# Hybrid DiT forward on one core: dead tiles as load buffers of the expert weights, row transposes one product later, routing in pieces

## The chip, the cores and the metric
One core of a Trainium2 chip runs the whole program. Its engines are PE (matrix products), ACT, DVE, POOL (element by element work, and POOL's indirect transfers) and SP, which issues the weight loads; 16 DMA engines move the data. The metric is the device time of one execution in microseconds (us); lower is better.

## The reference
Two transformer layers on 512 latent tokens of width 1024 and 256 context tokens, all in float32. Layer 0 mixes by a convolution and neighbourhood attention and has a dense feed-forward. Layer 1 mixes by windowed and differential attention, and its feed-forward is a mixture of eight experts, of which each token takes two. The change touches the second half of layer 1:

```python
def swiglu(x, w1, w3, w2):
    return (jax.nn.silu(x @ w1) * (x @ w3)) @ w2
...
    logits = (xt @ router).astype(jnp.float32)
    top_v, top_i = lax.top_k(logits, TOP_K)
    top_w = jax.nn.softmax(top_v, axis=-1)
    gates = jnp.sum(jax.nn.one_hot(top_i, N_EXPERTS, dtype=jnp.float32) * top_w[..., None], axis=1)
...
    for e in range(1, N_EXPERTS):
        out = out + gates[:, e:e + 1] * swiglu(xt, w1[e], w3[e], w2[e])
...
        h = h + g1 * y
        h = h + g2 * ffn(rms_norm(h, norm2_g[l]) * (1 + sc2) + sh2)
```
An expert has w1 and w3 of 1024 x 1408 and w2 of 1408 x 1024.

## The kernel before
**Numbers in halves.** Each float32 weight block is split into two float16 halves, `whi` on ACT (line 269) and the rest `wlo` on DVE (line 274); PE forms three float16 products for each block of 128 rows (`mm1`, line 342).

**The weight stream.** `Stream` walks a list of blocks in the order in which PE wants them. An expert has 11 blocks `m13` (128 x 2048, 1 MB, two tiles of w1 and w3) and 8 blocks `m2` (128 x 1408, 704 KB). `load_to` issues loads on SP (line 246) into buffers of the kind 'st'; `split_to` makes the halves in buffers of the kind 'hl', and each split issues the load that may use the place; `get` splits up to `ls` blocks ahead of PE (5 among the experts). The buffer of block i follows from i modulo their number. Among the experts there are five 'st' (two of the pool, `wst`, two of a further pool, `wstx`, and a third of the dead normed-activation tile `aT3`) and eight 'hl' (four, two `whix`/`wlox`, and two thirds of `aT3`). A buffer's name in a row is that of the pool or tile that it lies in, so a row `aT<-wst` is a split too. Blocks in the set `fine` are split in four pieces of 512 columns.

**The norm and the routing.** Behind the attention's output product the residual `h` is complete; the sum of its squares (ACT, line 453) goes through a small chain for the root on DVE (lines 321 to 333), then `n` is formed on DVE and ACT (lines 421, 419), and PE transposes it (`nps`, line 431) and computes the router's logits. `route` then ranks the tokens on DVE: eight fixed places ("slots") with capacities 176, 192, 96, 176, 112, 152, 136 and 128 take the eight experts. For each slot one-hot rows `ohs` (line 1684) and small PE products (`idxps`) give the token of each place; `idx`, the target row `sidx` and the weight `ws` follow by small DVE operations for each slot and half, and `cmax` (line 1790) says whether any expert has more tokens than places. SP reads `cmax` in its queue (line 1904) to decide on an overflow loop, which doesn't run on these inputs.

**An expert.** Its rows come from memory by indirect transfers on POOL (`gather`, line 1796; `xg`), are transposed by PE (`xtp`, line 1821), scaled (`xaf`, line 1825) and split into `xT`; this `prep` for expert e+1 is issued after block j = 6 of expert e. For expert 0, PE makes `xT` by products with one-hot rows instead (line 1817). Then eleven blocks j: 48 products each into a PSUM tile `mps` (three buffers), emptied one block later by `evac`: ACT's silu `ms` (line 1847), DVE's `mgf` (line 1848), and for j = 3, 7, 10 the halves `mgT` (lines 1853, 1854). Then eight blocks d of w2: 33 products each, and `evac2`: ACT's `my` (line 1876), PE's transposes `ytp` (line 1880), DVE's weighting into `yr` (line 1884). After d = 7, in the last expert after d = 4 and d = 7, POOL adds the rows to the result in memory (line 2019). A capacity over 128 needs two row halves: 128 and the rest.

**What sets the order.** The program order is that of the code, rearranged by a scheduler that fills each engine's instruction list; each engine then runs its list in order, and waits where an operand isn't there.

## Time and profile before
| | us |
|---|---|
| three runs, median (lowest to highest) | 1785.67 (1781.9 to 1789.2) |
| the profiled execution | 1788.69 |
| its span, first to last instruction | 1786.8 |
| PE busy in the span | 1668.7 |
| DVE busy in the span | 1251.0 |
| ACT busy in the span | 883.1 |

The mean granted TensorE clock of the profiled execution is 0.977. The span is what the rows below are counted in; what lies around it is 1.9 us. Busy time of an engine is a sum over stages with different limits, so it is read stage by stage.

### The profile page before, as it was taken

The numbers are of one execution on the slowest core, as the hardware profiler recorded it, in microseconds if no ns is written. First come the engines' busy times: TensorE is split into PE (matmuls) and PEld (weight loads), VectorE is DVE, ScalarE is ACT, GpSimd is POOL, SyncE is SP. The second block draws the span as 40 slices with busy tenths as digits, with TensorE's granted clock in tenths as the row PEclk, the third lists the DMA queues.
The fourth block names the chain that finished last, engine by engine and source line by source line (L and its number), as shares of the span: only waits on it lengthen the run. The fifth ranks groups of instructions, "written<-read, shape, count | busy, mean of one in ns | idle before, by whom it ended". The sixth has DMA issues, their size and how long they took to land. (4 is left out here: it accounts for less than half of the span.)

```text
span 1786.8 us, 36195 instructions
## 1 busy us (share of the span) xinstructions
PE 1668.7 (93%) x15124; PEld 1170.3 (65%) x15124; DVE 1251.0 (70%) x2463; ACT 883.1 (49%) x1420; POOL 156.1 (9%) x102
## 2 busy tenths in 40 slices
PE   3999999999999999999999999989789999999997
PEld 1444666555566665555555466447579988989997
DVE  6784899877665444333147999696898588788884
ACT  6564555262222222111254667564666577677773
POOL 1100000000000000000000000451210113101201
PEclk9999999999999999999999999999799999999999
DMA  8413342534333442233312201101569788899893
GB/s 322 160 51 100 104 166 95 212 117 143 142 129 131 142 142 96 73 112 112 115 61 79 95 1 48 70 3 54 189 204 337 240 312 334 303 330 336 313 337 109
DMA packets 51801, 286.82 MB, mean 161 GB/s; under 512 B 5824, under 2 KB 10944, under 8 KB 27568
## 3 DMA queue, kind: packets, MB, share of 16 engines
q1 hardware_dynamic: 47328, 271.74, 41.8%
q0 software_dynamic: 3296, 10.95, 2.7%
q8 instruction: 120, 1.97, 0.4%
q10 hardware_dynamic: 1008, 1.77, 0.3%
q14 instruction: 49, 0.40, 0.1%
HBM read 272.57 MB, written 11.08 MB: 159 GB/s over the span
## 5 line engine op out<-in xcount | busy, mean ns | idle before, releaser
L342 PEld LDWEIGHTS <-whi 128*128 128x128 f16 x5184 | 469.7, 99 | 185.3 <-issue 10.8
L342 PE MATMUL f<-yT,whi 128*128 128x512 f16 (+1 forms) x1408 | 325.5, 326 | 1.5 <-ACT af L438 1.5
L342 PEld LDWEIGHTS <-wlo 128*128 128x128 f16 x2592 | 255.6, 99 | 90.4 <-issue 2.2
L274 DVE SCALAR_TENSOR_TENSOR wlo<-wst,whi 128x512 f16<-128x512 f32 (+2 forms) x154 | 236.8, 1549 | 68.1 <-ACT whi L269 67.6
L269 ACT ACTIVATE whi<-wst 128x2048 f16<-128x2048 f32 (+2 forms) x152 | 199.4, 1331 | 111.1 <-PE f L342 72.8
L342 PE MATMUL f<-yT,wlo 128*128 128x512 f16 (+1 forms) x704 | 229.1, 326 | 0.0
L375 DVE SCALAR_TENSOR_TENSOR adjk<-wst,srow 128x1024 bf16<-128x1024 f32 x96 | 117.3, 1221 | 98.4 <-DMA wst<-in_w_adr_dram 97.2
L342 PE MATMUL f<-gT,whi 128*128 128x512 f16 (+1 forms) x704 | 164.4, 326 | 0.0
L342 PE MATMUL mps<-xT,whi 128*128 128x176 f16 (+6 forms) x1472 | 149.0, 229 | 3.8 <-DVE mgf L1848 3.7
L342 PE MATMUL mps<-xT,wlo 128*128 128x176 f16 (+6 forms) x736 | 143.0, 229 | 0.0
L342 PE MATMUL f<-gT,wlo 128*128 128x512 f16 (+1 forms) x352 | 114.7, 326 | 0.0
L342 PEld LDWEIGHTS <-aT 128*128 128x128 f16 x1584 | 106.8, 99 | 5.3 <-issue 4.5
L467 DVE TENSOR_TENSOR h<-h,ytp 128x256 f32<-128x256 f32 (+1 forms) x48 | 24.3, 507 | 109.2 <-PE ytp L465 108.9
L2019 POOL DMA_INDIRECT out_dram<-yr,sidx x14 | 54.4, 3885 | 358.3 <-DVE yr L1884 215.3
L342 PE MATMUL cvps<-aT,whi 128*128 128x512 f16 (+1 forms) x384 | 82.6, 328 | 2.8 <-ACT Kl L632 2.3
L342 PEld LDWEIGHTS <-whix 128*128 128x128 f16 x992 | 81.4, 98 | 2.9 <-issue 2.5
L1082 ACT CAST gT<-g 128x512 f16<-128x512 f32 (+1 forms) x23 | 14.0, 608 | 131.0 <-DVE g L1079 131.0
L274 DVE SCALAR_TENSOR_TENSOR wlo<-wstx,whi 128x2048 f16<-128x2048 f32 (+2 forms) x42 | 68.7, 1651 | 14.0 <-ACT whi L269 11.4
L342 PE MATMUL mps<-xT,aT 128*128 128x176 f16 (+6 forms) x1056 | 74.4, 231 | 2.3 <-DVE mgf L1848 2.3
L342 PE MATMUL mps<-mgT,whi 128*128 128x176 f16 (+6 forms) x704 | 73.0, 227 | 0.9 <-ACT mgT L1853 0.9
L342 PE MATMUL mps<-mgT,wlo 128*128 128x176 f16 (+6 forms) x352 | 68.1, 227 | 0.0
L269 ACT ACTIVATE whi<-wstx 128x2048 f16<-128x2048 f32 (+2 forms) x42 | 57.7, 1401 | 17.6 <-PE mps L342 16.3
(398 smaller groups left out, 3490.1 us busy)
## 6 DMA issues: line engine op xcount, KB each, us to landing
wst<-in_w_m_dram SPq DMA_DIRECT2D x38, 1024.0 KB, 6.2
wstx<-in_w_m_dram SPq DMA_DIRECT2D x33, 1024.0 KB, 6.2
wst<-in_w_adr_dram SPq DMA_DIRECT2D x32, 1024.0 KB, 4.9
wst<-in_w_f_dram SPq DMA_DIRECT2D x22, 1024.0 KB, 4.8
wst<-in_w_m_dram SPq DMA_DIRECT2D x27, 704.0 KB, 6.0
wstx<-in_w_m_dram SPq DMA_DIRECT2D x25, 704.0 KB, 6.1
aT<-in_w_m_dram SPq DMA_DIRECT2D x17, 1024.0 KB, 6.2
wst<-in_w_ada_dram SPq DMA_DIRECT2D x12, 1024.0 KB, 4.9
```

Of the source, the lines that this page charges most:

```text
L269: nc.scalar.activation(h, x, AF.Copy, scale=self.scale)
L274: nc.vector.scalar_tensor_tensor(out=l, in0=x, scalar=SW, in1=h, op0=OP.mult, op1=OP.subtract)
L342: mm(ps[:, s0:s0 + sn], w[:, k, :], a[:, kk, s0:s0 + sn], start=first and p == 0, stop=last and p == 2)
L375: nc.vector.scalar_tensor_tensor(out=jk, in0=st[:, j * D:(j + 1) * D], scalar=1.0, in1=self.srow[:, t, :], op0=OP.mult, op1=OP.mult, accum ...
L467: nc.vector.tensor_tensor(out=hs, in0=hs, in1=tp[:, 0:w].rearrange("p (t c) -> p t c", t=nt), op=OP.add)
L1082: nc.any.tensor_copy(gh, g[:, 0:sn])
L2019: self.nc.gpsimd.indirect_dma_start(out=to, out_offset=bass.IndirectOffsetOnAxis(ap=self.sidx[0:sn, e, s:s + 1], axis=0), in_=yr[0:sn, s, ...
```

## The change
Five things are edited.

1. **Load buffers.** The tiles of the queries `Qc` and of the keys `Kd`, dead after the attention, are kept and serve as three 'st' buffers as soon as the differential attention is done; behind the routing the dead residual tile `h` gives three more. All three parts of `aT3` become 'hl' buffers, the further pool gives one 'hl' alone. That makes eight of each kind (2 + 3 + 3, and 4 + 1 + 3). A block takes the buffer that was used longest ago.
2. **Even halves.** A capacity over 128 is cut in two equal halves (88 + 88, 96 + 96, 76 + 76, 68 + 68), each with a `yr` tile of its own.
3. **Rows later.** `evac2` only makes `my`; the transposes and `yr` (now `rows`) come one block d later.
4. **Split start of w2.** Products of d = 0 and d = 1 run over k = 0 to 7 first, then over k = 8 to 10.
5. **Routing in pieces.** Only slots 0 and 1 are done ahead of expert 0. The one-hot rows of the others, the targets and weights of all slots in one go, and `cmax` (`excess`) are called from expert 0's loop over j (`beside`).

```diff
     def slot(self, i, kind, cols):
-        n = self.ns if kind == 'st' else self.nb
-        more = self.more.get(kind, []) if i < self.more_end else []
-        r = i % (n + len(more)) - n
-        if r >= 0 and more[r] is not None:
-            return [z[:, 0:cols] for z in more[r]]
-        pool, n, x = (self.pool, n, '') if r < 0 else (self.more_pool, more.count(None), 'x')
+
+        e = min((z for z in self.slots[kind] if z[0] == 'base' or i < self.more_end), key=lambda z: z[2])
+        where, pool, last = e
+        e[2] = i
+        if where not in ('base', 'pool'):
+            assert last < (self.nsplit if kind == 'st' else self.pos), (kind, i, last)
+            return [z[:, 0:cols] for z in pool]
+        x = '' if where == 'base' else 'x'
+        n = sum(z[0] == where for z in self.slots[kind])
...
-            T['cq'] = lp.tile([128, 8, NL], F16, name="Qc")
+            T['cq'] = self.kp.tile([128, 8, NL], F16, name="Qc")
             T['ck'] = lp.tile([128, 3, NT], F16, name="Kc")
-            T['dk'] = lp.tile([128, 12, NT], F16, name="Kd")
+            T['dk'] = self.kp.tile([128, 12, NT], F16, name="Kd")
...
+                qk = [T['cq'].rearrange("p a t -> p (a t)")]
+                kd = T['dk'].rearrange("p a t -> p (a t)")
+                qk += [kd[:, 4 * D * z:4 * D * z + 4 * D] for z in range(2)]
+                self.wfix = [fixed_slot('st', f"qk{i}", z) for i, z in enumerate(qk)]
+                self.S.extend(fixed=self.wfix)
+                self.S.load_to(self.S.nsplit + self.S.depth())
...
-        for s in range(1, NE):
-            tokens(s, slots(s, lambda t: ps_[:, s - 1, t:t + 1]))
-            if s == 1:
-                self.gather(1)
...
+        tokens(1, slots(1, lambda t: ps_[:, 0, t:t + 1]))
+        for i, (s0, sn) in enumerate(self.slots[1]):
+            V.tensor_copy(self.idx[0:sn, 1, i:i + 1], ip[0:sn, 1, i, 0:1])
+        self.gather(1)
+
+        def rest(j):
+
+            if j == 0:
+                tokens(0, first)
+            elif 2 <= j + 1 < NE:
+                s = j + 1
+                tokens(s, slots(s, lambda t: ps_[:, s - 1, t:t + 1]))
+                if s == 2:
+                    for i, (s0, sn) in enumerate(self.slots[s]):
+                        V.tensor_copy(self.idx[0:sn, s, i:i + 1], ip[0:sn, s, i, 0:1])
+            elif j + 1 == NE:
+
+                to = rp.tile([128, 8, 2], F32, name="to")
+                V.tensor_copy(self.idx[:, 3:NE, :], ip[:, 3:NE, :, 0])
+                V.tensor_scalar(to, ip[:, :, :, 1], -1.0, 1.0, op0=OP.mult, op1=OP.add)
+                V.tensor_tensor(out=to, in0=to, in1=own.unsqueeze(2).broadcast_to([128, 8, 2]), op=OP.mult)
+                V.tensor_tensor(out=to, in0=to, in1=ip[:, :, :, 0], op=OP.add)
+                V.tensor_scalar(to[:, NE - 1, :], to[:, NE - 1, :], 8.0, None, op0=OP.mult)
+                V.tensor_copy(self.sidx, to)
+                V.tensor_reduce(out=self.ws, in_=ip[:, :, :, 2:4], axis=AX.X, op=OP.add)
+            elif j == NE:
+                excess()
...
+            if beside is not None:
+                beside(j)
...
-        yr = mp.tile([128, max(2, len(slots)), D], F32, name="yr", tag="yr", bufs=1)
+        yr = [mp.tile([128, D], F32, name="yr", tag=f"yr{s}", bufs=1) for s in range(len(slots))]
         py = []
 
         def evac2():
             d, ps = py.pop(0)
-            y = mp.tile([128, cm], F32, name="my", tag="my", bufs=2)[:, 0:C]
+            y = mp.tile([128, cm], F32, name="my", tag="my", bufs=nb)[:, 0:C]
             nc.scalar.activation(y, ps[:, 0, 0:C], AF.Copy, scale=gate[:, d, 0:1])
+            ys.append((d, y))
+
+        def rows():
+            d, y = ys.pop(0)
             tp = pp.tile([128, max(2, len(slots)), 128], F32, name="ytp", tag="t", bufs=2)
             dd = slice(d * 128, (d + 1) * 128)
             for s, (s0, sn) in enumerate(slots):
                 nc.tensor.transpose(tp[0:sn, s, :], y[:, s0:s0 + sn], self.ident)
                 if wt is None:
-                    nc.vector.tensor_copy(yr[0:sn, s, dd], tp[0:sn, s, :])
+                    nc.vector.tensor_copy(yr[s][0:sn, dd], tp[0:sn, s, :])
                 else:
-                    nc.vector.tensor_scalar(yr[0:sn, s, dd], tp[0:sn, s, :], wt[0:sn, s:s + 1], None, op0=OP.mult)
+                    nc.vector.tensor_scalar(yr[s][0:sn, dd], tp[0:sn, s, :], wt[0:sn, s:s + 1], None, op0=OP.mult)
             done(d, yr)
 
+        def part(w, ps, ks):
+            for k in ks:
+                self.mm1(ps[:, 0], *w, k, gT[:, 0], gT[:, 1], seg, k == 0, k == 10)
+
+        ys = []
+        w0 = []
         for d in range(8):
-            wh, wl = (z.rearrange("p (k c) -> p k c", k=11) for z in w2(d))
+            if d > 1 and len(ys) > nb - 1:
+                rows()
+            w = [z.rearrange("p (k c) -> p k c", k=11) for z in w2(d)]
             ps = pp.tile([128, 2, CB], F32, name="mps2", tag="m", bufs=3)
-            for k in range(11):
-                self.mm1(ps[:, 0], wh, wl, k, gT[:, 0], gT[:, 1], seg, k == 0, k == 10)
+            if d < 2 and nb > 1:
+
+                part(w, ps, range(8))
+                w0.append((w, ps))
+                if d == 0:
+                    continue
+                for i in range(2):
+                    part(*w0[i], range(8, 11))
+                    py.append((i, w0[i][1]))
+                evac2()
+                continue
+            part(w, ps, range(11))
             if py:
                 evac2()
             py.append((d, ps))
         evac2()
+        while ys:
+            rows()
...
-        self.slots = [[(0, min(C, 128))] + ([(128, C - 128)] if C > 128 else []) for C in CAPS]
+
+        self.slots = [[(0, C // 2), (C // 2, C // 2)] if C > 128 else [(0, C)] for C in CAPS]
         self.eid = {}
...
-            self.S.extend(wx, 2, 2)
+            self.S.extend(wx, 0, 1, fixed=self.wfix)
...
-                self.S.extend(wx, 2, 2, fixed=[fixed_slot(k, z) for k, z in zip(BUSE, B)])
+                H = [self.ht[:, 2 * D * z:2 * D * z + 2 * D].bitcast(F16) for z in range(3)]
+                self.S.extend(wx, 0, 1, fixed=self.wfix + [fixed_slot('hl', f"a{i}", z) for i, z in enumerate(B)]
+                              + [fixed_slot('st', f"h{i}", z) for i, z in enumerate(H)])
```

`excess` holds the removed lines from `cb` to `cmax`, unchanged. Line numbers in the rows of the changed order are those of the changed file, 14 to 63 higher.

What moves is seen at three places of the engines' lists. First DVE at the norm ahead of the routing; `sst` is the sum of squares, `rs_v`, `rs_r` and `rs_t` the chain of the root, `n_3` the normed rows. Before:

```order
L324 TENSOR_SCALAR rs_v<-rs_v 128x2 [waits DVE_49]
L329 SCALAR_TENSOR_TENSOR rs_t<-rs_r,rs_v 128x1 [waits DVE_49]
L329 SCALAR_TENSOR_TENSOR rs_t<-rs_r,rs_v 128x1
L333 SCALAR_TENSOR_TENSOR rs_r<-rs_t,rs_r 128x2 [waits DVE_49]
L329 SCALAR_TENSOR_TENSOR rs_t<-rs_r,rs_v 128x1 [waits DVE_49]
L329 SCALAR_TENSOR_TENSOR rs_t<-rs_r,rs_v 128x1
L333 SCALAR_TENSOR_TENSOR rs_r<-rs_t,rs_r 128x2 [waits DVE_49]
L329 SCALAR_TENSOR_TENSOR rs_t<-rs_r,rs_v 128x1 [waits DVE_49]
L329 SCALAR_TENSOR_TENSOR rs_t<-rs_r,rs_v 128x1
L333 SCALAR_TENSOR_TENSOR rs_r<-rs_t,rs_r 128x2 [waits DVE_49]
L421 TENSOR_SCALAR n_3_13519<-h_11895,rs_r 128x512 [waits DMAHW1_49,DMAHW2_49,DVE_49,Pool_49]
```

And of the change, from the same instruction on:

```order
L338 TENSOR_SCALAR rs_v<-rs_v 128x2 [waits DVE_49]
L288 SCALAR_TENSOR_TENSOR wlo_14097<-Qc,whi_14096 128x512 [waits DMAHW1_49,Activation_49]
L343 SCALAR_TENSOR_TENSOR rs_t<-rs_r,rs_v 128x1 [waits DVE_49]
L343 SCALAR_TENSOR_TENSOR rs_t<-rs_r,rs_v 128x1
L288 SCALAR_TENSOR_TENSOR wlo_14097<-Qc,whi_14096 128x512 [waits Activation_49]
L347 SCALAR_TENSOR_TENSOR rs_r<-rs_t,rs_r 128x2 [waits DVE_49]
L288 SCALAR_TENSOR_TENSOR wlo_14097<-Qc,whi_14096 128x512 [waits Activation_49]
L343 SCALAR_TENSOR_TENSOR rs_t<-rs_r,rs_v 128x1 [waits DVE_49]
L343 SCALAR_TENSOR_TENSOR rs_t<-rs_r,rs_v 128x1
L288 SCALAR_TENSOR_TENSOR wlo_14097<-Qc,whi_14096 128x512 [waits Activation_49]
L347 SCALAR_TENSOR_TENSOR rs_r<-rs_t,rs_r 128x2 [waits DVE_49]
```

Four pieces of a split of a weight block (in `Qc`; block 7 of expert 0) now stand inside the chain; three instructions of the root and `n_3` follow. ACT's list at the same place, of the change:

```order
L467 ACTIVATE sqj,ssq_11906<-h_11901 128x128 [waits DVE_49,Activation_49]
L467 ACTIVATE sqj,ssq_11906<-h_11901 128x128 [waits Activation_49]
L283 ACTIVATE whi_14096<-Qc 128x512 [waits DMAHW1_49]
L283 ACTIVATE whi_14096<-Qc 128x512 x3
L433 ACTIVATE n_3_13527<-h_11901,rs_r 128x512 [waits DMAHW4_49,DMAHW5_49,DVE_49,Pool_49]
L433 ACTIVATE n_3_13527<-h_11901,rs_r 128x512
```

The first two rows are the last sums of squares, and `n_3` is ACT's part of the normed rows; before, nothing stood between them. The four pieces of `whi` moved in, the first with a wait for a transfer.

Second, PE in expert 0. Of the change:

```order
L356 MATMUL mps<-xT,whi_13259 128x176
L356 LDWEIGHTS whi_13351
L356 MATMUL mps<-xT,whi_13351 128x176
L1858 MATMUL xtp<-ident,xg_13924 128x96 [waits DMASW4_49]
L1858 MATMUL xtp<-ident,xg_13924 128x96
L356 LDWEIGHTS whi_13171
L356 MATMUL mps<-xT,whi_13171 128x176 [waits DVE_49]
L356 LDWEIGHTS wlo_13172
L356 MATMUL mps<-xT,wlo_13172 128x176
```

`xg` are the gathered rows of expert 1, `xtp` their transposes. These two stand behind the first 39 products of expert 0 (`mps<-xT`), with a wait for the gather. Before, all sixteen stood behind block j = 2:

```order
L342 MATMUL mps<-xT,whi_13342 128x176
L342 LDWEIGHTS wlo_13343
L342 MATMUL mps<-xT,wlo_13343 128x176
L1821 MATMUL xtp<-ident,xg_13918 128x128 [waits DMASW4_49,Activation_49]
L1821 MATMUL xtp<-ident,xg_13918 128x64 [waits DMASW5_49]
L1821 MATMUL xtp<-ident,xg_13918 128x128
L1821 MATMUL xtp<-ident,xg_13918 128x64
L1821 MATMUL xtp<-ident,xg_13918 128x128 [waits Activation_49]
```

Fourteen of the sixteen moved back, behind block j = 6, and two moved forward.

Third, ACT behind the routing, of the change (`sw` is the scale of a split, `xaf` and `xT` the operand of expert 0):

```order
L283 ACTIVATE whix_13930<-Kd,sw 128x512 x2
L1862 ACTIVATE xaf<-xtp,nB_106,nA_102 128x176 [waits PE_49]
L283 ACTIVATE whix_13930<-Kd,sw 128x512
L1865 CAST xT<-xaf 128x704 [waits DVE_49,Activation_49]
L1862 ACTIVATE xaf<-xtp,nB_106,nA_102 128x176 [waits PE_49]
L283 ACTIVATE aT_13066<-Kd,sw 128x512 x2
L1862 ACTIVATE xaf<-xtp,nB_106,nA_102 128x176 [waits PE_49]
L283 ACTIVATE aT_13066<-Kd,sw 128x512 x2
L283 ACTIVATE aT_13066<-wst_13181,sw 128x512 x4
L1865 CAST xT<-xaf 128x704 [waits DVE_49,Activation_49]
```

The second CAST of `xT`, which was on DVE before, stands here behind the pieces of splits of blocks 4 and 5.

## Rows read from the trace of the kernel before
**Rows 1.** The page, parts 1 and 2: busy time of each engine, and the bytes moved in 40 equal slices of 44.7 us each. The expert part is slices 29 to 40.
```profile
PE 1668.7 (93%) x15124; PEld 1170.3 (65%) x15124; DVE 1251.0 (70%) x2463; ACT 883.1 (49%) x1420; POOL 156.1 (9%) x102
GB/s 322 160 51 100 104 166 95 212 117 143 142 129 131 142 142 96 73 112 112 115 61 79 95 1 48 70 3 54 189 204 337 240 312 334 303 330 336 313 337 109
```

**Rows 2.** Stretches of 50 us of the expert part, all engines. Columns: stretch, length, then busy us (and number of instructions) of PE, PEld, DVE, ACT, POOL, the granted TensorE clock, the DMA share, GB/s.
```profile
1300.00:1350.00 50.00, 43.66 (x507) 41.02 (x506) 45.66 (x152) 30.97 (x44) 6.13 (x5) 0.90 0.73 245
...
1450.00:1500.00 50.00, 45.01 (x823) 41.09 (x822) 38.80 (x44) 37.23 (x49) 8.49 (x4) 0.90 0.89 310
...
1700.00:1750.00 50.00, 48.57 (x802) 46.79 (x800) 44.82 (x50) 37.02 (x42) 4.41 (x2) 1.00 0.94 337
```

**Rows 3.** Waits of PE between 1255 and 1787 us: who waited <- for whom: us in total, times, longest us.
```profile
PE mps L342 <- DVE mgf L1848: 8.7, 8, 3.7
PE ytp L1880 <- ACT my L1876: 5.4, 12, 1.1
...
PE mps L342 <- ACT mgT L1853: 1.9, 5, 0.5
PE ytp L1880 <- DVE yr L1884: 1.9, 8, 0.4
```

**Rows 4.** PE's timeline, places in expert 0 and the begin of its second product (`mgT`). Columns: start us, us, engine, line, operation, out<-in, count, and in brackets the idle time before and what ended it.
```profile
1313.00 3.35 PE L1821 MATMUL xtp<-ident,xg 128*128 128x128 f32 x12 [0.19 <-ACT xaf L1825]
1318.47 3.82 PE L342 MATMUL mps<-xT,aT 128*128 128x176 f16 x25 [2.12 <-DVE mgf L1848]
...
1339.04 0.31 PE L342 MATMUL mps<-xT,whi 128*128 128x176 f16 x2 [3.75 <-DVE mgf L1848]
...
1355.24 1.98 PE L342 MATMUL mps<-mgT,aT 128*128 128x176 f16 x24
```

**Rows 5.** Stretches of 5 us, columns as in rows 2.
```profile
1310.00:1315.00 5.00, 4.67 (x39) 3.44 (x37) 5.00 (x52) 2.19 (x5) 0.00 (x0) 1.00 0.01 3
...
1335.00:1340.00 5.00, 1.25 (x17) 1.11 (x15) 5.00 (x5) 4.12 (x7) 0.00 (x0) 0.99 0.77 246
1340.00:1345.00 5.00, 5.00 (x47) 5.00 (x45) 5.00 (x6) 2.97 (x3) 0.00 (x0) 0.67 0.92 297
1345.00:1350.00 5.00, 5.00 (x69) 5.00 (x67) 3.80 (x5) 3.40 (x5) 0.00 (x0) 1.00 0.94 330
...
1475.00:1480.00 5.00, 5.00 (x64) 4.91 (x65) 3.06 (x4) 3.10 (x6) 2.49 (x2) 0.51 0.72 254
1480.00:1485.00 5.00, 5.00 (x121) 5.00 (x118) 3.42 (x4) 3.94 (x5) 0.00 (x0) 1.00 0.70 224
```

**Rows 6.** Groups of instructions between 1240 and 1360 us. Columns: line, engine, operation, out<-in, out<-in shapes, count, then busy us, mean ns of one, idle before.
```profile
L274 DVE SCALAR_TENSOR_TENSOR aT<-wst,aT 128x512 f16<-128x512 f32 x8 | 5.2, 676 | 0.0
...
L1848 DVE SCALAR_TENSOR_TENSOR mgf<-mps,ms 128x176 f32<-128x176 f32 x11 | 3.6, 335 | 1.7 <-ACT ms L1847 1.7
...
L274 DVE SCALAR_TENSOR_TENSOR wlo<-wstx,whi 128x2048 f16<-128x2048 f32 x1 | 2.3, 2285 | 0.0
...
L1684 DVE TENSOR_SCALAR ohs<-cstm,pms 128x128 f16<-128x128 f32 x4 | 0.9, 273 | 0.0
...
L269 ACT ACTIVATE whi<-wst 128x512 f16<-128x512 f32 x16 | 9.1, 624 | 3.6 <-DMA wst<-in_w_m_dram 2.4 <-PE odps L342 1.2
```

**Rows 7.** Timelines of DVE and PE at the norm ahead of the routing, columns as in rows 4.
```profile
1273.22 0.16 DVE L476 TENSOR_REDUCE sst<-ssq 128x2 f32<-128x6 f32 x1 [0.30 <-ACT sqj L453]
...
1275.57 0.16 DVE L333 SCALAR_TENSOR_TENSOR rs_r<-rs_t,rs_r 128x2 f32<-128x2 f32 x1
1275.82 0.88 DVE L421 TENSOR_SCALAR n<-h,rs_r 128x512 f32<-128x512 f32 x2
...
1276.45 1.09 PE L431 MATMUL nps<-ident,n 128*128 128x128 f32 x4 [3.22 <-DVE n L421]
```

**Rows 8.** SP's timeline and its wait, which hold the load queue (SPq); the first rows as in rows 4, the last as in rows 3.
```profile
1267.91 0.33 SPq L246 DMA_DIRECT2D wst<-in_w_m_dram  x1
...
1299.23 0.33 SPq L246 DMA_DIRECT2D aT<-in_w_m_dram  x1
1315.45 3.07 SPq L246 DMA_DIRECT2D wst<-in_w_m_dram  x2
...
SPq L1904 <- DVE cmax L1790: 13.8, 1, 13.8
```

**Rows 9.** PE's and ACT's timelines where expert 2 (96 places) runs, columns as in rows 4.
```profile
1467.73 1.38 ACT L269 ACTIVATE aT<-wstx 128x1408 f16<-128x1408 f32 x1 [1.83 <-DMA wstx<-in_w_m_dram]
1469.55 0.71 PE L1821 MATMUL xtp<-ident,xg 128*128 128x128 f32 x2 [1.42 <-ACT xaf L1825]
```

**Rows 10.** POOL's timeline at the first gather, columns as in rows 4, and from the view of the tile `xg` the time from issue to landing of all 11 gathers (1300 to 1591 us).
```profile
1300.22 1.24 POOL L1796 DMA_INDIRECT xg<-n_d,idx  x1 [12.62 <-DVE ohs L1684]
...
DMA to landing us min/median/max: 4.6/5.8/8.4
```

**Rows 11.** Timelines of DVE and POOL at the end of the last expert, columns as in rows 4.
```profile
1769.29 0.35 DVE L1884 TENSOR_SCALAR yr<-ytp,ws 128x128 f32<-128x128 f32 x1 [1.61 <-PE ytp L1880]
1771.24 0.35 DVE L1884 TENSOR_SCALAR yr<-ytp,ws 128x128 f32<-128x128 f32 x1 [1.60 <-PE ytp L1880]
...
1771.88 1.59 POOL L2019 DMA_INDIRECT out_dram<-yr,sidx  x1 [27.11 <-DVE yr L1884]
1778.05 1.56 POOL L2019 DMA_INDIRECT out_dram<-yr,sidx  x1 [4.58 <-DMA out_dram<-yr,sidx]
```

106 lines of the change are left out of this document (55 added, 51 removed).

## The prediction
> **What bounds the kernel now.** I began with the busy times. PE works 93% of the span, DVE 70%, ACT 49% [rows 1], so PE is the bound wherever it doesn't stop, and a change that leaves its matmuls alone can only give back PE's stops and the time it spends at a low clock. The edit leaves everything up to about 1250 us in its order, so the question is the expert part alone, 1297 to 1776 us. Read in stretches of 50 us [rows 2], a good one has 48.57 us of PE; only two fall short: 1300 to 1350 (43.66, granted clock 0.90) and 1450 to 1500 (45.01, clock 0.90). DMA is close behind PE in the good ones (337 GB/s, share 0.94), so in this part the weight stream is the second bound.
>
> Then the waits of PE by name [rows 3]: `mgf` 8.7 us in 8 stops, of which two in expert 0 make 2.12 and 3.75 [rows 4]; the row transposes `ytp` behind ACT's `my` 5.4 us in 12; behind DVE's `yr` 1.9; `mgT` 1.9. After a stop the clock falls: behind the 3.75 us the next 5 us hold 47 matmuls at clock 0.67, against 69 at full clock [rows 5]. Who is late in expert 0 is DVE: it is busy 5.00 of 5 us from 1310 to 1315, with 52 small instructions of the routing, and again from 1335 to 1345 with the splits [rows 5]. SP's load queue stands 13.8 us behind the count `cmax` [rows 8]: no load leaves between 1299.23 and 1315.45, and DMA moves 3 GB/s in 1310 to 1315 [rows 5].
>
> **Expert 0.** In the new order DVE loses 78 instructions, nearly all from the routing chain; at 52 in 5.00 us [rows 5], 96 ns each, that is 7.5 us. The one-hot rows of slots 2 to 7 and `cmax` move into the loop, one slot per block: 4 `ohs` of 273 ns [rows 6]. A block then costs DVE 2285 + 335 + 4 x 273 = 3.7 us against PE's 48 matmuls at 5.00/69 = 72 ns, 3.5 us. The two run neck and neck, so a stop like that of 3.75 us should go, but a reserve isn't built.
>
> Against that, PE's order has two transposes of expert 1's gathered rows after the first 39 matmuls, about 1302 us, where before all stood later, behind block 2. They wait for the gather. It leaves at 1300.22 and lands 5.8 us later, the median of eleven [rows 10]; nothing makes it leave earlier. So PE stands from 1302 to 1306.2, and by the row behind the 3.75 us stop it then loses (69 - 47) x 72 ns = 1.6 us to the clock. The second cast of `xT`, now on ACT behind pieces of splits at 624 ns [rows 6], is ready at about 1303.4, inside that stop; without the stop it would hold PE up for 1.4 us. What is left of blocks 0 to 2 is 105 matmuls, 7.6 us, and 1 us of the matmuls that place the tokens: block 3 begins at 1316.4, against 1318.47 [rows 4]. DVE has its first `mgf` by then or slightly earlier: 16 split pieces of 676 ns [rows 6] stand ahead of it, 10.8 us from about 1301 on, and two groups of `ohs`. From block 3 on: 8 x 48 x 72 ns = 27.8 us, 14 transposes at 3.35/12 = 0.28 us [rows 4], 3.9, and 1.3 for placing tokens: 33.0, end 1349.4 against 1355.24 [rows 4]. That is -5.8 us, if the start stays.
>
> The start doesn't stay. ACT's and DVE's splits of block 7, whose load now goes to the place of Qc, stand ahead of the last norm. That load leaves with the one now seen at 1267.91 [rows 8]; with five to six us of flight it lands at about 1273 to 1274. ACT's sums end at 1273.2 [rows 7]; then four pieces at 624 ns [rows 6], 2.5 us, and DVE's four at 676 ns, each behind ACT's, then the rest of the root, about 0.9 us: `n` at 1277.9 if the load is there at 1273.2, at 1279.3 if it comes with 1.4 us delay. Before: 1275.82 [rows 7]. Everything behind it, the router and the first product, follows: +2.1 to +3.5 us; I take +2.9, near the middle, as the load is in a queue with others. **Expert 0: -5.8 + 2.9 = -2.9 us.** Ends: if the gather is landed in time, PE's stop (4.2) and its clock (1.6) go too and the delay is 2.1: -9.5. If the gather lands behind other traffic, or DVE falls behind by a few blocks at 0.2 us plus handoffs: +1.
>
> One thing speaks against the 5.8 us: this gather shared the DMA engines with one weight block (that of 1299.23), since SP then stood behind `cmax` [rows 8], and in the new order more loads leave meanwhile. The longest of the eleven, most of them beside a full weight stream, took 8.4 us [rows 10]; then the stop ends at 1308.6 and expert 0 gives -0.5 instead of -2.9 us. A rule makes it more: the Trainium skill, DMA: Bandwidth & Descriptors, section Issuing engines are not separate DMA queues, says that transfers issued by different engines run on the same 16 DMA engines and interleave; behind three whole weight blocks it would be 9.3 us by the rate in rows 2, and expert 0 would give +0.4. The trace's median of 5.8 beside that stream speaks for less, and the sum goes by it.
>
> **Expert 2.** With 96 columns it uses up weights faster than they come. ACT waits 1.83 us for a block, its scaling of the transposed rows (`xaf`) stands behind that, and PE stops 1.42 us [rows 9]. The clock is at half for about 10 us behind it: 64 matmuls in 1475 to 1480 against 121 in the next 5 us [rows 5], that is 57 x 41 ns = 2.4 us per 5 us, 4.7 in all. Eight load buffers instead of five put 3 blocks more in reserve, 3 x 1.05 MB at 337 GB/s = 9.3 us, more than the 1.83 us of lateness. All 6.1 us could go; transposes that wait for ACT stay, so **-5.5 us**. Ends: -6.5 and 0, the latter if the reserve is used up before: the stream needs 8 x 17.3 = 138 MB (11 blocks of 1.05 and 8 of 0.72 for an expert) at 337 GB/s, 411 us of the 479 that the expert part lasts, so it isn't short on the whole.
>
> **The rows.** The transposes of a block of 128 outputs now come one block later, so ACT's `my` has a whole product (33 matmuls) of slack. Of 5.4 us [rows 3] I take **-4.5**; the `yr` waits (1.9) stay, since DVE's writes still free the PSUM tile of two. Ends: -6 and -2. The split of products 0 and 1 after `k` = 7 looks like a cure for the waits on `mgT` and the rest of `mgf` (1.9, and 8.7 - 2.12 - 3.75 = 2.8), but before had interleaved these products nearly so already: **-1**, ends -3 and 0.
>
> **The end.** In the last expert the five transposes that release the first scatter come one product later: 1771.24 minus 1769.29 = 1.95 us [rows 11]. The second scatter waits for the landing of the first (4.58 us at 1778.05 [rows 11]), so the end moves with it: **+1.9 us**; ends 0 and +2.
>
> Even row halves cost nothing: as many scatters, gathers and transposes, 96 + 96 rows for 128 + 64, off PE's path by the same products. The added memset of the PSUM tile of the token places is one small DVE instruction, 0.1 us [rows 5], ahead of the routing's end; it is inside the roundings.
>
> **Sum.** -2.9 - 5.5 - 4.5 - 1 + 1.9 = -12.0. The profiled execution took 1788.69 (span 1786.8), so 1776.7; it lies 3.0 above the median of 1785.67 of the three runs. From the median it would be 1773.7. I say 1775.
>
> **Rivals.** *More*: the gather lands before PE gets there, as DVE is slower than PE and holds PE up in blocks 0 and 1 anyway. Expert 0 gives -9.5 and with the rest -18.6: 1768. For it: DVE is full from 1310 to 1315 [rows 5]. Against: 39 matmuls need only 3 us from 1299 on.
>
> *Swallowed*: gather slow beside the weight stream (expert 0 -0.5), and half of the `my` waits stay, as waits for `yr` (-2.2): -0.5 - 5.5 - 2.2 + 1.9 = -6.3, 1779 to 1782 by the two bases, too little to be told: of this kernel a measurement tells some 0.5%, 9 us, from no change.
>
> *The deeper reserve does nothing*, because transfers are limited by bandwidth and not by buffers in expert 2: -12.0 + 5.5 = -6.5, 1779 to 1782. Against: 1300 to 1350 moves only 245 GB/s [rows 2], so that there is reserve to be built.
>
> *Slower*: PE falls to half clock at the gather and isn't kept busy enough by DVE to leave it. Expert 0's blocks 2 to 7, 6 x 3.5 = 21 us, would then take up to 21 more. From 12 us on the kernel is slower than before; with all 21 it stands at 1796. For it: half clock (0.51) for 10 us followed a stop of only 1.42 [rows 5, 9]. Against: after 3.75 us the clock was back to 1.00 in 10 us [rows 5].
>
> The Trainium skill's page TensorE: Matmul & The Clock Gate, section HAM oscillation, says that a wait for a transfer ahead of each group of matmuls keeps the clock low over and over. By that rule it would be the slower case, with its 1796; the trace shows a drop of one or two 5 us stretches only.
>
> **How the numbers follow.** Forecast (1770 to 1780) 0.38; more 0.22; swallowed 0.16; reserve does nothing 0.10; slower 0.14. Faster by over 0.5% means below 1776.7: all of *more* and three quarters of the forecast, 0.50. Slower by over 0.5% means above 1794.6: nearly all of *slower*, 0.13. The rest, 0.37, is the same: the two middle rivals, a quarter of the forecast, a little of *slower*. The range goes down to 1761, where *more* stands with the better ends of expert 2, the rows and the split products (-1, -1.5, -2) and a run 2.5 under the median, and up to 1790, where it takes in the two middle rivals, expert 0 at its worse end and the run-to-run height of 1789.2, and leaves *slower* out.
>
> **What would show it.** `n` of the last norm 2 to 3.5 us later against the routing's first matmuls; an idle of 4 us at the first `xtp` of expert 1, ended by DMA; no `cmax` wait on SP; block 3 at about 1319, end of expert 0's first product at 1352; 1470 to 1480 at full clock; waits of `ytp` on `my` under 1 us; the first of the last scatters one product later in its expert. I am wrong if DVE, not the gather, ends PE's stops in expert 0, if the clock in 1300 to 1350 stays below 0.90, or if ACT still waits for loads in expert 2.

## The result and the profile after

The changed kernel took 1797.55 us (median; 1795.93 to 1801.08), the kernel before 1785.67 (1780.23 to 1789.2) in runs beside it. The ratio is 1.0074, with an interval of 1.0054 to 1.0095: slower by 0.7%, where 1775 was forecast. The profiled execution has a span of 1795.8 us, 9.0 more than before (1786.8).

The page's first part, busy time of each engine:

```profile
PE 1654.4 (92%) x15124; PEld 1164.0 (65%) x15124; DVE 1244.4 (69%) x2397; ACT 882.2 (49%) x1420; POOL 155.0 (9%) x103
```

PE does the same 15124 matmuls in 14 us less busy time than in [rows 1], and yet the span is longer. PE is idle for 23 us more. So the loss is idle time. Stretches of 50 us, columns as in [rows 2]:

```profile
1300.00:1350.00 50.00, 35.57 (x462) 34.77 (x460) 36.21 (x88) 26.49 (x39) 15.12 (x4) 0.86 0.62 209
...
1450.00:1500.00 50.00, 44.97 (x890) 42.70 (x888) 44.76 (x52) 40.06 (x53) 5.87 (x4) 1.00 0.94 298
1700.00:1750.00 50.00, 38.40 (x612) 37.16 (x610) 35.49 (x39) 30.57 (x32) 5.63 (x2) 0.90 0.76 254
```

1300 to 1350 has 8 us less PE than before, and 1700 to 1750, a good stretch in [rows 2], has 10 less. Only 1450 to 1500, expert 2, improved: the same PE time, but 890 matmuls instead of 823, at full clock. In the first row POOL is busy 15.12 us where it was 6.13; that number leads to the cause.

PE's waits by name, 1200 to 1796 us, columns as in [rows 3]:

```profile
PE ytp L1923 <- DVE yr L1927: 15.6, 15, 10.3
PE xtp L1858 <- DMA xg<-n_d,idx: 13.0, 1, 13.0
PE nps L445 <- DVE n L435: 5.3, 2, 5.1
PE ytp L1923 <- ACT my L1915: 3.8, 5, 1.5
...
PE mps L356 <- DVE mgf L1885: 2.1, 6, 0.9
```

Two single stops, 13.0 and 10.3 us, are new; together they are the 23 us. `mgf` went from 8.7 to 2.1 and `my` from 5.4 to 3.8. By the first and last matmul of each product in the two traces (first product `xT`, second `mgT`), in us:

| | before | after | difference |
|---|---|---|---|
| expert 0 begins | 1297.0 | 1299.0 | +2.0 |
| expert 0, first product | 58.4 | 61.9 | +3.5 |
| expert 2, first / second | 34.2 / 15.5 | 27.3 / 14.9 | -6.9 / -0.6 |
| expert 4, second | 17.6 | 15.4 | -2.2 |
| expert 6, second | 19.4 | 30.5 | +11.1 |
| last matmul of the products to the span's end | 11.8 | 14.8 | +3.0 |

All other products lie within 1.6 us of before. The table is of one execution of each kernel.

**The first stop.** PE's, POOL's and DVE's timelines (columns as in [rows 4]) around the first gather:

```profile
1318.76 0.58 PE L1858 MATMUL xtp<-ident,xg 96*128 96x96 f32 x2 [13.05 <-DMA xg<-n_d,idx]
...
1302.23 11.73 POOL L1833 DMA_INDIRECT xg<-n_d,idx  x1 [13.40 <-DVE idx L1778]
1314.26 0.92 POOL L1833 DMA_INDIRECT xg<-n_d,idx  x1 [0.30 <-issue]
...
1301.94 1.88 DVE L288 SCALAR_TENSOR_TENSOR wlox<-Kd,whix 128x512 f16<-128x512 f32 x3
1303.74 1.88 DVE L288 SCALAR_TENSOR_TENSOR aT<-Kd,aT 128x512 f16<-128x512 f32 x3
1305.55 0.88 DVE L1866 TENSOR_TENSOR xT<-xaf,xT 128x704 f16<-128x704 f32 x1
1306.35 0.68 DVE L288 SCALAR_TENSOR_TENSOR aT<-Kd,aT 128x512 f16<-128x512 f32 x1
1306.95 4.89 DVE L288 SCALAR_TENSOR_TENSOR aT<-wst,aT 128x512 f16<-128x512 f32 x8
1311.77 1.31 DVE L1707 TENSOR_SCALAR ohs<-cstm,pms 128x128 f16<-128x128 f32 x6
```

Before, POOL issued this gather in 1.24 us [rows 10]; now its instruction lasts 11.73, and it ends 0.9 us after DVE's chain of splits and one-hot rows does. The next half, issued behind it with DVE idle, takes 0.92. From issue to landing the first half took 16.5 us.

**The second stop.** PE, DVE and POOL where expert 6's second product runs:

```profile
1677.40 12.78 POOL L2085 DMA_INDIRECT out_dram<-yr,sidx  x1 [58.03 <-DVE mgf L1885]
1707.90 1.82 POOL L2085 DMA_INDIRECT out_dram<-yr,sidx  x1 [17.71 <-DVE mgT L1891]
...
1724.78 0.60 DVE L1927 TENSOR_SCALAR yr<-ytp,ws 68x128 f32<-68x128 f32 x2 [10.13 <-DMA out_dram<-yr,sidx]
...
1725.44 0.43 PE L1923 MATMUL ytp<-ident,my 128*68 128x128 f32 x1 [10.33 <-DVE yr L1927]
```

Expert 5's two scatters are late: the first needs 12.78 us to be issued and lands 29.6 us after its begin, at 1707.0; the second begins behind that landing and lands at 1724.7. DVE may write expert 6's rows into the one `yr` tile of a half only when expert 5's scatter has read it. DVE waits 10.13 us for that DMA, and PE for DVE.

**The norm and the end.** ACT's pieces of block 7, and DVE's `n` behind them; then the last scatters on POOL:

```profile
1272.54 2.17 ACT L283 ACTIVATE whi<-Qc 128x512 f16<-128x512 f32 x4
...
1277.17 0.88 DVE L435 TENSOR_SCALAR n<-h,rs_r 128x512 f32<-128x512 f32 x2
...
1779.79 1.58 POOL L2085 DMA_INDIRECT out_dram<-yr,sidx  x1 [21.06 <-DVE yr L1927]
1785.80 1.56 POOL L2085 DMA_INDIRECT out_dram<-yr,sidx  x1 [4.43 <-DMA out_dram<-yr,sidx]
```

`n` is at 1277.17 instead of 1275.82 [rows 7], 1.35 us later.

### The profile page after: what moved, and what is told of

Its sections match the earlier page's. It is cut to its first block, busy times and chain, and to the rows that moved or that the text cites. A ratio compares the mean times of both kernels' runs of the same rounds, so it can differ in the third digit from the quotient of the medians.

```text
span 1795.8 us, 36123 instructions
## 1 busy us (share of the span) xinstructions
PE 1654.4 (92%) x15124; PEld 1164.0 (65%) x15124; DVE 1244.4 (69%) x2397; ACT 882.2 (49%) x1420; POOL 155.0 (9%) x103
## 5 line engine op out<-in xcount | busy, mean ns | idle before, releaser
L288 DVE SCALAR_TENSOR_TENSOR wlo<-wst,whi 128x2048 f16<-128x2048 f32 (+2 forms) x113 | 172.3, 1534 | 53.9 <-ACT whi L283 53.7
L283 ACT ACTIVATE whi<-wst 128x2048 f16<-128x2048 f32 (+2 forms) x115 | 147.0, 1299 | 89.0 <-PE f L356 71.9
L356 PEld LDWEIGHTS <-aT 128*128 128x128 f16 x2376 | 153.6, 98 | 2.7 <-issue 2.2
L356 PE MATMUL mps<-xT,whi 128*128 128x176 f16 (+6 forms) x1408 | 142.3, 228 | 1.6 <-ACT xT L1865 1.3
L288 DVE SCALAR_TENSOR_TENSOR wlo<-h,whi 128x2048 f16<-128x2048 f32 (+1 forms) x54 | 107.2, 1987 | 21.2 <-ACT whi L283 18.4
L283 ACT ACTIVATE whi<-h 128x2048 f16<-128x2048 f32 (+1 forms) x54 | 90.2, 1672 | 48.4 <-PE mps L356 46.6
L356 PE MATMUL mps<-xT,aT 128*128 128x112 f16 (+6 forms) x1584 | 105.5, 225 | 0.0
L288 DVE SCALAR_TENSOR_TENSOR aT<-wst,aT 128x2048 f16<-128x2048 f32 (+2 forms) x44 | 76.2, 1749 | 12.5 <-ACT aT L283 12.4
L283 ACT ACTIVATE aT<-wst 128x2048 f16<-128x2048 f32 (+2 forms) x40 | 62.3, 1569 | 23.2 <-PE mps L356 22.0
L2085 POOL DMA_INDIRECT out_dram<-yr,sidx x14 | 41.9, 2989 | 336.6 <-DVE yr L1927 184.9
```

The source lines that it names most:

```text
L283: nc.scalar.activation(h, x, AF.Copy, scale=self.scale)
L288: nc.vector.scalar_tensor_tensor(out=l, in0=x, scalar=SW, in1=h, op0=OP.mult, op1=OP.subtract)
L356: mm(ps[:, s0:s0 + sn], w[:, k, :], a[:, kk, s0:s0 + sn], start=first and p == 0, stop=last and p == 2)
L2085: self.nc.gpsimd.indirect_dma_start(out=to, out_offset=bass.IndirectOffsetOnAxis(ap=self.sidx[0:sn, e, s:s + 1], axis=0), in_=yr[s][0:sn, ...
```

## Experiments

All edits are made on the changed kernel, some of them on top of `gap0`; ratios are to the kernel before, in runs on the same chip. Only the last one leaves out a part of the computation.

**What holds up PE in expert 0.** `xtp_after` keeps the first gathered transpose of each expert in its written place; all sixteen then stand behind block 6 (336 products).

```diff
-                    nc.tensor.transpose(tp[:, s0:s0 + sn], xg[0:sn, s, ...
+                    q = nc.tensor.transpose(tp[:, s0:s0 + sn], xg[0:sn, s, ...
+                    if k == 0 and s == 0:
+                        self.tc.keep_in_program_order(q)
```

> The changed kernel with one edge of order: the first transpose of the next expert's gathered rows may not move ahead of block 6's products on PE. The gather itself is left as it is. Theory (a late gather stops PE only because two transposes were moved to the front): the 13.0 us stop goes, and with it some 2 us of low clock, but DVE's first mgf, near 1327 in the changed kernel because PE stood, comes near 1314, so that PE may stop 1 to 3 us there: 1784 to 1788 against 1797.5. The POOL instruction of the first gather stays at 11 to 12 us, since DVE still runs the same 16 split pieces beside it. Rival (the stop was DVE's, and the gather only the last of several): a stop on mgf of 10 us or more takes its place, 1794 to 1799.

Measured: 1783.58 us, ratio 0.9988 (0.9977 to 0.9999). The stop is gone and expert 0's first product takes 48.6 us; the issue stays long, and so does the wait for `yr` (9.8 us in one stop). POOL's timeline:

```profile
1301.97 10.97 POOL L1833 DMA_INDIRECT xg<-n_d,idx  x1 [13.38 <-DVE idx L1778]
```

So the long issue isn't a consequence of PE's stop, and it costs time only where PE waits for the rows. DVE, which the forecast had neck and neck with PE, holds PE up 2.1 us in all here.

**What makes the issue long.** `gap0` lets POOL fill a small tile right behind the first half's gather; DVE's splits (block 7 apart) read their scale from it, so that they can't begin before the gather is issued. The two transposes, too, stand behind block 2 again in this kernel, where PE comes to them at 1312.1.

```diff
+        z = self.ms.tile([128, 1], F32, name="flag", tag="flag", bufs=2)
+        self.tc.keep_in_program_order(self.nc.gpsimd.memset(z, SW))
+        self.S.lo = z
...
-                    nc.vector.scalar_tensor_tensor(out=l, in0=x, scalar=SW, in1=h, ...
+                    nc.vector.scalar_tensor_tensor(out=l, in0=x, scalar=SW if key == ('m13', 0, 7) else self.lo, in1=h, ...
```

> The changed kernel, where DVE's splits of expert 0 behind block 2 (but that of block 7) read their scale from a small tile which POOL fills right after it has issued the first half of the gather, so that none of them can run beside that issue. The scheduler then also puts the first transposes behind block 2 again. Theory A (POOL's issue of an indirect transfer stands still while DVE runs two-input instructions back to back): the POOL instruction of the first gather takes 1 to 2 us instead of 11.7 and the rows land within 6 us of it; no stop of PE on the gather; 1783 to 1788. Theory B (the weight loads that now run beside it delay the gather): the loads are the same, so the instruction stays at 8 to 12 us or its landing comes 15 us or later, and PE still stops on the gather for several us: 1792 to 1798. The second half of the gather is a control within the run: it is issued beside the split pieces, and by theory A stays long (5 to 12 us).

Measured: 1774.22 us, ratio 0.9943 (0.9927 to 0.996), better than either number. POOL and DVE:

```profile
1301.88 1.17 POOL L1839 DMA_INDIRECT xg<-n_d,idx  x1 [13.37 <-DVE idx L1779]
...
1303.35 0.93 POOL L1839 DMA_INDIRECT xg<-n_d,idx  x1 [0.19 <-DVE xT L1874]
1304.59 1.45 POOL L1839 DMA_INDIRECT xg<-n_d,idx  x1 [0.30 <-DVE ohs L1708]
...
1302.30 0.89 DVE L1874 TENSOR_TENSOR xT<-xaf,xT 128x704 f16<-128x704 f32 x1
...
1304.51 2.73 DVE L289 SCALAR_TENSOR_TENSOR wlox<-Kd,flag,whix 128x512 f16<-128x512 f32 x4
```

The issue fell to 1.17 us; this half landed 5.9 us after its issue began, at 1307.8, well ahead of PE. DVE was busy all through the 1.17 us, with casts, a one-hot row and the `xT` row above, which reads two tensors too, but with no split piece. The control, a second half that stays long, missed: the pieces began only at 1304.51, behind it. The third gather then did what the control was for, and it speaks against theory A as worded: it took 1.45 us although the pieces ran beside it, and so it did (1.45 to 1.48 us) in the six other kernels that hold this edit. So keeping the pieces away makes the issue short, but pieces beside an issue don't always make it long. Traffic doesn't make it long, as a row of stretches for each kernel shows (columns as in [rows 2]); the 0.93 us issue in this kernel, then the 11.73 us one in the changed kernel:

```profile
1303.35:1304.28 0.93, 0.93 (x15) 0.93 (x13) 0.30 (x2) 0.93 (x3) 0.93 (x1) 1.00 1.02 432
```

```profile
1302.23:1313.96 11.73, 2.15 (x30) 1.79 (x28) 10.85 (x22) 5.13 (x9) 11.72 (x1) 0.77 0.83 294
```

The short one had the busier DMA engines (432 against 294 GB/s), the long one the busy DVE (10.85 of 11.73 us). The wait for `yr` went as well without having been aimed at (4.0 us, longest 1.1): expert 5's first scatter took 3.91 us to be issued here, not 12.78. What order did that was not followed up.

**Which part of the change puts them together.** `route_first` does all slots' routing ahead of expert 0, as before.

```diff
-        return rest
+        for j in range(NE + 1):
+            rest(j)
+        return None
```

> The changed kernel with the routing's pieces called ahead of expert 0 again, in the new, shorter form (one-hot rows of all slots, targets and weights in one go, the count). All else is as in the changed kernel: eight buffers, even halves, rows one product later. Theory (spreading the routing is what put the run of 16 split pieces beside the gather): small one-hot instructions stand on DVE there instead, the POOL instruction of the first gather takes 1 to 3 us, and PE doesn't stop on the gather; 1780 to 1788, with DVE late for the first mgf by some us in its place. Rival (the run comes from the eight buffers, which have blocks 3 to 6 landed early): the instruction stays above 8 us and the time at 1792 to 1798.

Measured: 1785.56 us, 1.0001 (0.9986 to 1.0016). No stop at the gather, and the first half's issue is short; POOL and DVE:

```profile
1303.20 1.32 POOL L1835 DMA_INDIRECT xg<-n_d,idx  x1 [13.37 <-DVE ohs L1707]
1304.83 3.80 POOL L1835 DMA_INDIRECT xg<-n_d,idx  x1 [0.30 <-issue]
...
1305.13 3.38 DVE L1707 TENSOR_SCALAR ohs<-cstm,pms 128x128 f16<-128x128 f32 x16
```

The second half took 3.80 us with no split piece beside it until its last 0.05 us: it ended 0.1 us behind a run of 16 one-hot rows, each of which reads one tensor and a scalar for each partition. With the routing's small instructions taken from in front of them, the splits had moved beside the gather. The wait for `yr` in expert 6 (9.2) is not tied to this.

**The second stop.** `yr2` gives the row halves two buffers each, and one 'hl' buffer less.

```diff
-        yr = [mp.tile([128, D], F32, name="yr", tag=f"yr{s}", bufs=1) for s in range(len(slots))]
+        yr = [mp.tile([128, D], F32, name="yr", tag=f"yr{s}", bufs=nb) for s in range(len(slots))]
...
-            self.S.extend(wx, 0, 1, fixed=self.wfix)
+            self.S.extend(wx, 0, 0, fixed=self.wfix)
```

> The changed kernel with two buffers for each half of yr, paid for with one of the eight buffers of halves. Theory (DVE's yr of expert 6 waits 10.1 us for a buffer that the slow second scatter of expert 5 still reads): that wait and the 10.3 us stop of PE go, with about 2 us of low clock: 1785 to 1788. Rival (the scatter's delay moves to another wait, or seven buffers of halves cost as much): 1793 to 1800. The slow issue of the scatter itself, 12.8 us on POOL, should stay under either.

Measured: 1785.16 us, 0.9994 (0.9982 to 1.0005). PE's waits, and the scatter of expert 5:

```profile
PE xtp L1858 <- DMA xg<-n_d,idx: 11.7, 1, 11.7
PE ytp L1923 <- DVE yr L1927: 6.9, 18, 0.8
```

```profile
1677.42 6.46 POOL L2085 DMA_INDIRECT out_dram<-yr,sidx  x1 [55.56 <-DVE mgf L1885]
```

The scatter is still slow, though half as long as expected (6.46 us for 12.8), but nobody waits for it; the stop at the gather stays. Each stop is taken out by itself, and each is worth 12 to 14 us by the medians.

**The norm.** `norm_first` keeps ACT's four pieces of block 7 in written order.

```diff
-                nc.scalar.activation(h, x, AF.Copy, scale=self.scale)
+                q = nc.scalar.activation(h, x, AF.Copy, scale=self.scale)
+                if key == ('m13', 0, 7):
+                    self.tc.keep_in_program_order(q)
```

> The changed kernel with the four split pieces of block 7 held behind the norm on ACT. Theory: the wait of the norm's transposes on n goes back from 5.1 to about 3.2 us, expert 0 begins 2 us earlier, and as the rest of the time is limited by the gather, which moves with it, the total gives 1.5 to 2.5 us: 1795 to 1796. Rival (the pieces only fill a gap): no gain, and block 7 is late in expert 0, +1 us or more: 1797 to 1800.

Measured: 1793.37 us, 1.0049 (1.0034 to 1.0063), 4.2 less than the changed kernel, though the two intervals touch. DVE's `n`:

```profile
1274.98 0.89 DVE L437 TENSOR_SCALAR n<-h,rs_r 128x512 f32<-128x512 f32 x2
```

2.2 us earlier; expert 0 begins at 1296.2, 2.8 earlier, and both stops stay (12.5 and 9.7).

**The load buffers.** `st5` is `gap0` without the three 'st' buffers on the residual.

```diff
-     + [fixed_slot('st', f"h{i}", z) for i, z in enumerate(H)])
+     )
```

> gap0 with five load buffers instead of eight behind the routing (the residual's tile isn't used; the halves' buffers stay eight). Theory (expert 2's first product takes 27.4 us instead of 34.2 thanks to the three more load buffers): expert 2 goes back towards 34 us, ACT waits for loads there again, 1779 to 1782. Rival (the eight buffers of halves, or the loads that now begin earlier, did it): expert 2 stays at 27 to 29 us and the time within 2 us of 1774.2.

Measured: 1794.34 us, 1.0059 (1.0036 to 1.0083). Expert 2's first product stayed at 27.5 us, as the rival had it, but the time didn't stay: expert 0 and experts 5 to 7 suffered most. ACT's longest waits from 1297 us on:

```profile
ACT whi L284 <- DMA Kd<-in_w_m_dram: 9.9, 7, 4.8
ACT whi L284 <- DMA Qc<-in_w_m_dram: 5.1, 1, 5.1
ACT whi L284 <- DMA wst<-in_w_m_dram: 4.8, 1, 4.8
```

ACT waits for loads 30.6 us in all, against 2.8 in `gap0` and 21.6 before. The three buffers are worth 20 us here, but not in expert 2's first product. What made that one faster than before is not shown: with five load buffers and eight of halves, as many as before, `st5` still has it.

**Rows one block later.** `nolag` is `gap0` with the rows right behind their product, as before.

```diff
-            if d > 1 and len(ys) > nb - 1:
+            if d > 1 and ys:
                 rows()
```

> gap0 with the row transposes of every expert right behind their product (the delay by one product undone; the split start of w2 stays). Theory (the delay is worth the stops on my that it takes away, about 4 us, less 1.9 at the end): the stops of ytp on my come back to 5 us or more, those on yr fall below 2.5 us, and the time is 1775 to 1778. Rival (the delay only trades stops on my for stops on yr): 1771 to 1774, as the end comes 1.9 us earlier.

Measured: 1770.31 us, 0.9929 (0.9913 to 0.9946), below the rival's 1771, though its interval overlaps that of `gap0`. The second products sum to 161.6 us against 158.6 in `gap0` (162.7 before), so late rows save 3.0 there. But the first products of experts 1 to 7 take nearly as much more in `gap0` (252.3 against 249.6): from the end of expert 0's first product to the last matmul it is 409.4 us with late rows, and 0.4 more without. Late rows lose 1.9 at the end, and another order put expert 0's end 2.7 us earlier here.

**Together.** `c1` is `gap0` with `norm_first` and early rows in the last expert alone; `c1y` adds `yr2`; `c3` is `gap0` with `norm_first` and early rows everywhere.

> gap0, and with it block 7's pieces held behind the norm, and the last expert's row transposes right behind their product as before the change (not one later). Theory: the three sums add: 1774.2 (gap0), -2.8 for the norm (expert 0 began 2.7 us earlier in that run), -1.9 for the last scatters: 1769 to 1771. Rival (what is gained at the start is lost again in expert 0, where DVE is full): the stops on mgf in expert 0 grow from 5.6 us in all, and the sum is 1771 to 1774.

> c1 with two buffers for each half of yr and seven of halves instead of eight. Theory (in c1 no scatter is late any more, as the stops on yr in gap0 were 4.0 us in all, the longest 1.1): no gain, 0 to +2 us against c1. Rival (the remaining stops on yr are on its buffer): 2 to 4 us less than c1.

> gap0, block 7's pieces held behind the norm, and the row transposes of every expert right behind their product: the version to which the runs so far point. If the parts add: 1774.2 - 3.1 (c1 with its end against gap0) and, as nolag came out 3.9 under gap0, 1768 to 1771. If the late rows are worth their 3 us in the second products once the start is the same: 1771 to 1774.

Measured: `c1` 1771.16 us, 0.9917 (0.9897 to 0.9937); `c1y` 1773.15, 0.9939 (0.9923 to 0.9956); `c3` 1771.4, 0.9914 (0.9893 to 0.9934). The parts don't add up: `c3` has nothing of `nolag`'s 3.9, since `norm_first` already brings the earlier expert 0 (its first product ends at 1346.2 in `c3`, at 1346.3 in `nolag`). `c1` and `c3` differ in the rows of experts 0 to 6 alone, late in `c1` and early in `c3`, and take the same time: late rows are worth nothing clear of noise. The second buffers of `c1y` add nothing. `c1` and `c3` are the best versions, 0.8 to 0.9% below the kernel before; `nolag` can't be told from them.

**No slow scatter at all.** `c3s` is `c3` with such a tile filled behind the first half of each scatter but the last, too.

```diff
+            if s == 0 and not last:
+                self.flag()
```

> c3, and each expert's first scatter (but the last expert's) is followed on POOL by the same small fill, which DVE's next splits read, so that no split runs beside the first half of a scatter. Theory (an issue lasts long only beside an unbroken DVE run): no POOL scatter over 5 us is left among the first halves, and since those of c3 stop nobody, the time is that of c3 or up to 3 us more, as DVE waits for POOL. Rival (something else than DVE makes them long): scatters of 6 to 13 us stay.

Measured: 1780.01 us, 0.9968 (0.9951 to 0.9985). No issue on POOL in the expert part lasts over 3.40 us, so the long issues are gone; but the time rises by 8.6 us over `c3`, where up to 3 were expected. PE's waits, and one of DVE's:

```profile
PE mps L359 <- DVE mgf L1896: 9.9, 12, 2.9
PE ytp L1934 <- ACT my L1926: 6.6, 13, 1.5
```

```profile
DVE wlo L291 <- POOL flag L1835: 6.3, 4, 2.0
```

DVE's splits wait 6.3 us for the small fills behind the scatters, and PE waits longer for DVE and ACT (5.2 for `mgf` and 5.1 for `my` in `c3`). That is half of the 13.0 us that lie between the spans of these two traces; the rest was not followed up. Holding splits back cost more here than long issues that nobody waits for.

**Which instructions of DVE.** `oneop` writes the 16 pieces beside the gather as scalings of one tensor; the low parts are then other numbers.

```diff
+                elif key in [('m13', 0, z) for z in (3, 4, 5, 6)]:
+                    nc.vector.tensor_scalar(l, x, SW, 1.0, op0=OP.mult, op1=OP.mult)
```

> The changed kernel, with DVE's 16 pieces of split of blocks 3 to 6 of expert 0 written as scalings of one tensor (weights times a constant) instead of scaling and subtracting a second tensor: the subtraction of the high part is left out, so these low parts are other numbers; everything else stays, the unbroken run of DVE beside the first gather too. Theory (POOL's issue of the gather is held by DVE instructions that read two tensors): the first gather's issue falls from 11.73 us to under 3 us, PE's stop at the first gathered transpose from 13.0 us to under 5 us, time 1786 to 1790 us. Rival (any DVE instructions back to back hold it): the issue still lasts until the run of pieces ends; as pieces get shorter than 610 ns it may be 5 to 11 us, its end within about 1 us of the end of the run, and the stop 7 us or more.

Measured: 1780.93 us in a single run (before beside it 1782.42), under the expected 1786 to 1790. POOL, and DVE beside it:

```profile
1302.38 1.33 POOL L1835 DMA_INDIRECT xg<-n_d,idx  x1 [13.90 <-DVE idx L1780]
1304.01 1.14 POOL L1835 DMA_INDIRECT xg<-n_d,idx  x1 [0.30 <-DVE aT L288]
...
1302.09 1.13 DVE L288 TENSOR_SCALAR aT<-wst 128x512 f16<-128x512 f32 x3
1303.13 0.46 DVE L1862 TENSOR_SCALAR xaf<-xtp,nA,nB 128x176 f32<-128x176 f32 x1
1303.50 0.43 DVE L288 TENSOR_SCALAR aT<-wst 128x512 f16<-128x512 f32 x1
1303.85 0.51 DVE L1867 CAST xT<-xaf 128x704 f16<-128x704 f32 x1
```

DVE has no gap beside the issue, and it takes 1.33 us; the stop is gone. So an unbroken run of DVE need not hold POOL's issue; the rival said that it does. That it is the two tensors is not shown: the order shifted in this kernel (four pieces lie beside the gather instead of sixteen), so that fewer pieces, shorter ones and one tensor instead of two are not told apart by it, and the 3.80 us in `route_first` lay beside rows that read one tensor.

## Why the prediction was wrong

**The step that failed is the gather in expert 0**: "It leaves at 1300.22 and lands 5.8 us later". That PE would stand at `xtp`, and that DMA would end the stop, was right; the stop was 13.0 us for 4.2. The flight was sized well (5.9 in `gap0`, where nothing holds the issue), but POOL's instruction was taken as the 1.24 us of [rows 10], and it lasted 11.73, so that the landing came 16.5 us after its begin. The prediction itself put 16 split pieces on DVE from about 1301 on, ahead of the first `mgf`, and never held them against POOL's issue. The SBUF page of the Trainium skill (SBUF — State Buffer, section SBUF: two separate sides) describes such a thing: transfers issued from GpSimd's queue have their descriptors written by GpSimd, which shares a port pair with VectorE and is shut out while certain VectorE instructions run, among them, against GpSimd work that reads SBUF, those with two SBUF inputs. The traces agree in part: 11.73 us beside the two-tensor pieces, 1.17 with none of them, 1.33 beside one-tensor pieces. The 1.45 us issue in `gap0` beside two-tensor pieces and the 3.80 us one in `route_first` beside one-tensor rows don't fit that reading. So it is shown that the run of pieces held this issue, and open which property of DVE's instructions does it. The rule that the prediction weighed, shared DMA engines, sized the wrong thing: it would have given 9.3 us.

**A term that wasn't there**: +10.3 in expert 6. The prediction kept the `yr` waits at 1.9, "since DVE's writes still free the PSUM tile of two", and looked at no scatter but the last. With one `yr` tile for a half, a scatter that is late by its issue (12.78) and a second that waits for the first reach the next expert's rows; `yr2`, with a second tile, has no `yr` wait over 0.8 us. Without this stop `yr` is 5.3 us, still 3.4 more than kept.

These two account for the miss: 13.0 - 4.2 + 10.3 = 19.1, and 1795.8 - 19.1 = 1776.7, against a forecast span of 1774.8. `gap0`, which has neither, has 1772.3. That the rest comes so near the forecast is in part luck: expert 2 and the norm came out better than their terms, the rows and the end worse.

**Expert 0 apart from the gather, "-5.8"**: better than sized. DVE, expected neck and neck with PE, holds PE up at `mgf` for 2.1 us in `xtp_after` and 5.6 in `gap0`, for 8.7 before, and with the gather out of the way the first product takes 48.6 to 50.2 us for 58.4. With the +2.0 of the norm that makes -6 to -8, between the -2.9 of the sum and the -9.5 of its good end.

**The norm, +2.9**: in mechanism right. `n` came 1.35 us later than before, under the forecast 2.1 to 3.5, and expert 0 began 2.0 later; `norm_first` brings `n` forward by 2.2 and expert 0 by 2.8.

**Expert 2, -5.5**: right in size, -6.9, at full clock, but not by the cause named; 1470 to 1480 us:

```profile
1470.00:1475.00 5.00, 4.74 (x95) 4.51 (x93) 5.00 (x6) 4.81 (x10) 0.00 (x0) 1.00 0.97 286
1475.00:1480.00 5.00, 5.00 (x110) 4.87 (x109) 4.29 (x8) 5.00 (x9) 2.91 (x2) 1.00 1.01 418
```

The prediction gave it to the three more load buffers. `st5` keeps expert 2's first product at 27.5 us without them and loses 20 us in all. So for that product the rival was right that the reserve does nothing, and the right number is luck; over the whole part the reserve is worth more than the forecast gave it. What sped expert 2 up stays open.

**The rows, -4.5**: too much. `my` waits fell by 1.6, not 4.5, and `yr` took over 3.4 of the wait; by `nolag`, and by `c1` beside `c3`, nothing clear of noise is left, since what the second products gain the first products lose. **The split start, -1**: no run undoes it. **The end, +1.9**: +3.0 in the tail; `nolag` gives back 1.9. **No `cmax` wait on SP**: right, none in SP's waits of 1250 to 1330.

**Slower**: this rival had 1796 by half clock behind the gather, in blocks where DVE doesn't keep PE busy enough to leave it. The time came true and the cause didn't: the loss was idle time. The sign that the prediction set for being wrong, a clock under 0.90 in 1300 to 1350, did come (0.86), but the half clock (0.50) lay in 1310 to 1320, where PE ran 1.24 us, and by 1325 it was back to 1.00. The 54 matmuls in 1320 to 1325 for some 73 in a full stretch are 1.4 us, as the forecast's 1.6.

## What to carry to other kernels

When an edit moves instructions on VectorE, ask what GpSimd issues in that stretch: here a run of split pieces made the issue of an indirect DMA ten times as long, and the wait appeared as a DMA's, on another engine. A single buffer that a transfer reads stops its next writer until the slowest transfer has read it, so reckon with the slowest issue in the trace and not with the median. Where an issue is late but nobody waits for it, leave it. And undo each part of a change in a run of its own: here the rows' gain in one product was lost in the next, and the load buffers paid in other experts than the one they were meant for.
